# Two-layer hybrid decoder step on one core: product C of the seven-product blocks in the small bank, its `up` made from a copy; three feed-forward blocks on the unnormed input; token mixing's loads and masks issued ahead of its layer norm

## The chip, the core and the metric

One core of a Trainium2 chip runs the whole program once. The metric is the device time of one execution in microseconds (us), and lower is better. The engines are called as the profile calls them: PE is TensorE's matmuls and PEld its weight loads, DVE is VectorE, ACT is ScalarE, POOL is GpSimd, and SP issues the DMAs. PE's granted clock is given as a share of 2.4 GHz, so 0.50 is 1.2 GHz.

## The reference, cut to what matters

The model has two layers and 1024 channels. The program computes 544 columns at once: 512 prompt positions and 8 sequences of 4 sampled positions.

```python
h = rmsnorm(x, g1)
# h @ w_in is shared out over four head groups of 256 channels each:
#  A gated delta rule      B short gated convolution
#  C windowed attention    D token mixing
# D: v = LayerNorm(gelu(.)); out = u * (tril(W_s) @ v + b) inside chunks of 128 positions
x = x + concat(A, B, C, D) @ w_out
h2 = rmsnorm(x, g2)
x = x + (silu(causal_dwconv3(h2 @ w_gate)) * (h2 @ w_up)) @ w_down   # 2816 hidden channels
```

## The kernel before, in words

**Matmuls.** An fp32 product is made as three passes of a narrower type. Each operand is split into a high part and a low part, and high times high, low times high and high times low are summed in PSUM. A product of 544 columns is done as two matmuls of 272 columns (`HT`). A weight tile comes by DMA (`wr`, 4 buffers, L709), ACT makes its high part (`wh`, L745, 3 buffers) and DVE its low part (`wl`, L747, 3 buffers).

**What sets the order.** PE's order is written by hand through the class `Order`. The main program is a generator, and the mixers are side generators (`a00`, `a10` for the delta rule, `c0`, `c1` for attention, `d0`, `d1` for token mixing). `Order.run` keeps an estimated time and picks whose step comes next. A side program yields a time or the name of an event, `mark(name, lat)` says when an event counts as ready, and the table `LAT` adds microseconds to single steps. The order of DVE, ACT, POOL and of SP's DMA queue is worked out by the tile framework's scheduler. Each engine, and SP's queue too, then runs its instructions strictly in that order.

**A layer.** It runs through these stages: the token-mixing and attention-value projections (`ptm`); nineteen 128-channel projections (`pj_*`), with the mixers' small matmuls slotted between their groups; the output product (`po`); the feed-forward net. Layer 1 has its mixers at 31 to 229 us and its feed-forward net at 281.5 to 666 us. Layer 2 has them at 689 to 887 and at 941.5 to 1335 us.

**Token mixing (group D).** `normed_dv` (L1525 to L1535) ends the layer norm: DVE scales the five `dvn`/`dvd` tiles (L1531), and POOL multiplies them by the gain and adds the bias (L1532, L1533). A DMA then writes `dvd` out (`o_cvs`, L1534), and the event `dv` is marked. `mix_d` (L1375) waits for that event first. Only then does it load the mixing weights `wmt` and `wm4` and the bias `dbias`, and POOL multiplies the weights by triangular masks (L1379, L1382). The mixing matmuls are `pmx` (prompt) and `pmd` (samples).

**Attention and delta rule.** `psc` are attention scores. They read `ck`, the rotated keys that DVE finishes at L1578. `pvt` are transposes of the delta rule.

**Feed-forward net.** It has 22 blocks of 128 hidden channels, each with a gate product `pgt` and an up product `pup`. There are three kinds of block:

- `raw` multiplies the unnormed input `xs`. DVE scales the results by `rstd` while it copies them out (L1713, L1714, L1716), and DVE multiplies by up at L1719. Blocks 0 and 1 are raw.
- `plain` multiplies normed forms `f1`, `f2`, `f3`, which `Forms.halves` makes on DVE and ACT (L578, L586, L587, L516). ACT copies the gate out of PSUM (L1728, L1729), and DVE multiplies by up at L1734. Blocks 2, 3 and 4 are plain.
- `seven` makes gate and up of one block from seven half-size products instead of eight (chains `pA`, `pB`, `pC`, `pD`). It reads sums of the forms (`Forms.sums`) and sums of the weights, which POOL makes (`wsums`: `s12` from L724 and L725, `s43` from L727 and L726). These sums stand behind the copy `sfo` of block 3 (L1695) on POOL. Blocks 5 to 21 are of this kind.

After some blocks the down products `pdn` run. Two PSUM pools matter here: `mm` (two buffers of two banks each: `pj`, `po`, `pgt`, `pup`, `pdn` and, before the change, `pC`) and `ps` (two buffers of one bank: `pA`, and the mixers' small results). A new product must wait until the engine that reads its buffer's previous tile is done.

Of the kernel before, what the change touches and what calls it, by code (L numbers as in the profile page):

```python
# [12 lines left out]
ALU = mybir.AluOpType  # L13
# [9 lines left out]
T = SEQ + ND  # L23
HT = T // 2
# [4 lines left out]
NK = DM // 128  # L29
EPS = 1e-6  # L30
FGROUPS = [(0, 5), (5, 11), (11, 17), (17, 22)]
RAW, PLAIN = 2, 5
P0 = 512 - HT


# [238 lines left out]
def _unhost(r):  # L274
# [8 lines left out]
    def conv(a, k, n):  # L283
# [19 lines left out]

LAT = {
    "a00": {
        3: 1.60, 13: 15.62, 14: 3.75, 15: 2.87, 16: 1.87, 17: 3.23, 18: 1.78, 19: 2.03, 34: 1.52,
    },
    "a01": {
        3: 3.96, 4: 1.12, 10: 2.64, 24: 0.84,
    },  # L310
    "a10": {
        3: 1.56, 13: 15.67, 14: 3.68, 15: 2.79, 16: 3.85, 17: 1.45, 25: 1.33, 36: 0.47, 42: 1.13,
    },
    "a11": {
        3: 3.59, 6: 3.32, 13: 1.06, 28: 0.70, 35: 0.30,
    },
    "c0": {
        1: 1.19, 2: 4.34, 5: 7.17, 6: 0.65, 7: 2.67, 8: 3.40,
    },
    "c1": {  # L320
        1: 0.81, 2: 4.06, 5: 7.68, 6: 0.61, 7: 15.38, 10: 1.48,
    },
    "d0": {
        4: 6.53,
# [90 lines left out]
def _body(ctx, tc, I, O, depth=DEPTH, dump=None):  # L415
# [6 lines left out]
    stt = dve.scalar_tensor_tensor  # L422
    od = Order()

    def mm(out, lhsT, rhs, **kw):
        k, m, n = lhsT.shape[0], lhsT.free_size(), rhs.free_size()
        if lhsT.dtype == F32R:
            c = max(n, 256) / 2400.0 + 0.0025
        else:
            c = 4 * max(n, m) / 2400.0  # L430
            if k <= 32 and m <= 32:
                c *= 0.74
            elif k <= 64 and m <= 64:
                c *= 0.72
        od.spend(c, n * k / 128.0 * (1 if lhsT.dtype == F32R else 4))
        nc.tensor.matmul(out, lhsT, rhs, **kw)  # L436
# [9 lines left out]
    def bc(ap, axis, n):  # L446
        u = ap.unsqueeze(axis)
        shp = list(u.shape)
        shp[axis] = n
        return u.to_broadcast(shp)  # L450
# [16 lines left out]
    def n5(nm, w=571):  # L467
        return p5.tile([128, w], F32, tag="w5", name=nm)

    def nx(nm, shape, dt=F32):  # L470
        return slabs.tile(shape, dt, tag="s5", name=nm)

    def ncc(nm, shape):
        return pc.tile(shape, F32, tag="c2", name=nm)
# [4 lines left out]
    def ps(nm, shape):  # L479
        return pss.tile(shape, F32, tag="ps", name=nm)  # L480

    def psmm(nm):
        return pmm.tile([128, 1024], F32, tag="mm", name=nm)
# [16 lines left out]
    def C(nm, a=None, b=None):  # L500
        o, n = _COFF[nm]
        if a is None:
            return cst[:, o:o + n]
        return cst[:, o + a:o + b]
# [280 lines left out]
    def dmp(nm, ap):  # L785
        if dump is not None and nm in dump:
            nc.gpsimd.dma_start(dump[nm], ap)

    def bs(ap):
        return ap.rearrange("p (b t) -> p b t", b=DB)  # L790
# [582 lines left out]


    def mix_d(l, L):  # L1375
        yield ("ev", f"dv{l}")
        wmt = nx("wmt", [128, 4, 128])
        nc.sync.dma_start(wmt, I["wmt"][l])
        pool.tensor_tensor(wmt, wmt, bc(C("tri"), 1, 4), op=ALU.mult)  # L1379
        wm4 = ncc("wm4", [32, 4, 32])  # L1380
        nc.sync.dma_start(wm4, I["wm4"][l])
        pool.tensor_tensor(wm4, wm4, bc(C("udc")[0:32], 1, 4), op=ALU.mult)  # L1382
        dbias = ncc("dbias", [128, 2, 128])
        nc.sync.dma_start(dbias, I["dbias"][l])
        for i in range(2):
            yield ("ev", f"u{l}{i}")
            pmx = ps("pmx", [128, 4, 128])
            for n in range(4):
                for a in range(2):
                    gr = 2 * i + a  # L1390
                    mm(pmx[hs[a], n], L.dvn[n // 2][:, n % 2, 64 * gr:64 * gr + 64], wmt[:, gr],
                       start=True, stop=True)
            pmd = ps("pmd", [128, ND])
            for a in range(2):
                gr = 2 * i + a
                mm(pmd[hs[a]], L.dvd[0:ND, 64 * gr:64 * gr + 64], wm4[:, gr], start=True, stop=True,
                   tile_position=(0, 64 * a))
            mx_ = n5("mx_", T)
            tt(mx_[:, 0:SEQ].rearrange("p (n t) -> p n t", n=4), pmx, bc(dbias[:, i], 1, 4), op=ALU.add)
            tt(bs(mx_[:, SEQ:T]), bs(pmd), bc(dbias[:, i, 0:DS], 1, DB), op=ALU.add)  # L1400
            tt(mx_, mx_, L.du[i], op=ALU.mult)
            dmp(f"od{i}", mx_)
            L.cat[6 + i] = split(mx_, f"d{i}")
            yield 1.0
        od.mark(f"catD{l}", 3.5)


    def main():
# [7 lines left out]
        def xk(k):  # L1416
            return xr[k // 2][:, k % 2, :]
# [33 lines left out]
        for l in range(depth):  # L1451
# [53 lines left out]
            for c in range(5):  # L1505
# [5 lines left out]
                dv = dvn[c // 2][:, c % 2] if c < 4 else dvd[0:ND]  # L1511
# [15 lines left out]
            def normed_dv():  # L1527
                yield ("ev", f"nd{l}")
                with tc.issue_after(L.du_ins):
                    for c, (dv, r0) in enumerate(dvs):  # L1530
                        ts(dv, dv, mv[0:r0, c, 0:1], rs[0:r0, c:c + 1], op0=ALU.subtract, op1=ALU.mult)  # L1531
                        pool.tensor_tensor(dv, dv, lnr[0:r0, 0], op=ALU.mult)  # L1532
                        pool.tensor_tensor(dv, dv, lnr[0:r0, 1], op=ALU.add)  # L1533
                nc.sync.dma_start(O["cvs"][l], dvd[0:ND])  # L1534
                od.mark(f"dv{l}", 8.0)  # L1535

            od.spawn(normed_dv(), f'n{l}')
            yield 0.0
# [199 lines left out]
            def seven(f):  # L1738

                B11, B21, B22, N1, N2, T3, N4 = fm.parts()  # L1740
                K = NK // 2
                a_ = ps("pA", [128, HT])
                b_ = psa.tile([128, HT], F32, tag="pa1", name="pB")
                d_ = psa.tile([128, HT], F32, tag="pa0", name="pD")
                sn = pd.tile([128, 4, HT], F32, tag="d5", name="sn")
                pb, dec = gate_in(f)
                n = SEQ - HT
                w = wnext()
                yield from chain(a_, w, 0, B11)
                act(sn[:, 0], a_, AF.Copy)  # L1750
                yield from chain(b_, w, K, B21)
                tt(pb[:, 2:2 + HT], b_, sn[:, 0], op=ALU.add)
                w = wnext()
                yield from chain(d_, w, 0, N1)
                act(sn[:, 1], d_, AF.Copy)
                yield from chain(a_, w, K, N2, start=False)
                act(sn[:, 2], a_, AF.Copy)
                w = wnext()
                yield from chain(d_, w, 0, B22, start=False)
                tt(pb[:, 2 + HT:2 + SEQ], d_[:, 0:n], sn[:, 2, 0:n], op=ALU.add)  # L1760
                tt(dec[:, :, 2:6], bs(d_[:, n:HT]), bs(sn[:, 2, n:HT]), op=ALU.add)  # L1761
                sl = gate_out(f, pb, dec)
                yield from chain(a_, w, K, T3, start=False)
                act(sn[:, 3], a_, AF.Copy)
                up = n5("up", T)
                stt(up[:, HT:T], a_, -1.0, sn[:, 1], op0=ALU.mult, op1=ALU.subtract)
                c_ = psmm("pC")[:, 0:HT]
                yield from chain(c_, wnext(), 0, N4)
                tt(up[:, 0:HT], c_, sn[:, 3], op=ALU.subtract)  # L1769
                tt(sl, sl, up, op=ALU.mult)  # L1770
                hid[f] = split(sl, "hd")
                yield 0.0

            for kind, i, f0, f1 in FFN_ORDER:
                if kind == "plain":
                    yield from raw(i, i == 0) if i < RAW else plain(i)
                    if i == 0:
                        for kp in range(NK // 2):
                            fm.halves(kp)
                    elif i == RAW:  # L1780
                        with tc.issue_after(fm.end.ins):
                            fm.sums()
                    continue
                if kind == "seven":
                    yield from seven(i)
                    continue
                m, last = i, f1 == NF
                hd = [hid[f] for f in range(f0, f1)]
                if last and l + 1 == depth and m >= NK - 2:
                    if m == NK - 2:  # L1790
                        yield from finale(xk, xr, nnrm, hd)
                    continue
                p = psmm("pdn")
                yield from gemm(p, wnext(), hd)
                tt(xk(m), xk(m), pflat(p), op=ALU.add)  # L1795
                if last:
                    if l + 1 < depth:
                        nx_xs.append(xsplit(xk(m), P(l + 1, "n1g", m, m + 1)))
                    nnrm.feed(m, xk(m))
                    if l + 1 == depth:  # L1800
                        act(xk(m), xk(m), AF.Copy, scale=fng[:, m:m + 1])
                yield 0.0
# [51 lines left out]
```

## Time and profile before

| what | value |
|---|---|
| median of 3 runs | 1336.76 us (1336.02 to 1337.26) |
| the profiled execution's own time | 1336.89 us |
| its span, first to last instruction | 1335.1 us |
| mean granted clock | 0.990 |
| PE busy | 1291.5 us (97%), 12574 matmuls |
| DVE busy | 958.9 us (72%) |
| ACT busy | 647.2 us (48%) |
| POOL busy | 401.9 us (30%) |

Busy shares are means over the span, and a wait is counted at the engine that waits. "[1.31 <-DVE ck L1578]" behind a row says that the engine stood idle for 1.31 us before it, and that DVE's write of `ck` at line 1578 ended that. The sum of PE's busy time holds slow stretches too: a matmul at clock 0.50 is busy for longer.

### The profile page before, as it was taken

Reading aid. Unit: us, or ns where it says so; the run is one execution under the profiler, and the core shown is the slowest. Engines: PE = TensorE matmul, PEld = TensorE weight load, DVE = VectorE, ACT = ScalarE, POOL = GpSimd, SP = SyncE. Lnnn points to the kernel's source line nnn. Section 1 sums busy time; section 2 is a strip of 40 time slices with the busy share of each in tenths; the row PEclk is TensorE's granted clock in tenths of the full one; section 3 lists DMA queues with packets and bytes.
Section 4 is the critical chain, followed back from the end, with each engine's and each line's share of the span. In section 5 each row is a group of like instructions: output and inputs, shape, how many; then the busy total and the mean of one; then the engine's idle time right before and its main releaser. Section 6 shows DMA issues by size and latency. Waiting matters only on the chain.

```text
span 1335.1 us, 29979 instructions
## 1 busy us (share of the span) xinstructions
PE 1291.5 (97%) x12574; PEld 1240.5 (93%) x12574; DVE 958.9 (72%) x1565; ACT 647.2 (48%) x1142; POOL 401.9 (30%) x528
## 2 busy tenths in 40 slices
PE   8998999999999999999999989999999999999997
PEld 7987889999999999999999878889989999999997
DVE  6897943579777778876658867546796887687665
ACT  6645423455455444544545543335555454455444
POOL 2123320001655354452001142100034654643321
PEclk9998999998999999999999989999999999999999
DMA  7222241231233233233532221413312332232232
GB/s 279 99 69 65 80 133 42 89 101 58 70 101 101 84 100 102 84 95 88 162 124 101 66 75 60 124 46 98 99 52 87 92 111 86 97 99 88 89 91 73
DMA packets 48086, 125.60 MB, mean 94 GB/s; under 512 B 10144, under 2 KB 14432, under 8 KB 47824
## 3 DMA queue, kind: packets, MB, share of 16 engines
q1 hardware_dynamic: 47952, 123.70, 29.6%
q8 instruction: 98, 1.61, 0.5%
q14 instruction: 36, 0.29, 0.1%
HBM read 115.01 MB, written 8.67 MB: 93 GB/s over the span
## 4 chain that ended last, share of the span: by engine, by line
PE 81%; DVE 11%; ACT 3%; issue 2%; DMA 1%; POOL 0%; SPq 0%; DVEq 0%; ACTq 0%; POOLq 0%
PE pdn L436 17%; PE pA L436 11%; PE po L436 8%; PE pD L436 7%; PE pup L436 4%; PE pgt L436 4%; PE pB L436 4%; PE pC L436 3%; DVE wl L747 3%; PE ptm L436 2%; PE pj_b L436 2%; PE pj_z L436 2%; PE pj_c L436 2%; PE pj_h L436 2%; PE p L436 2%
## 5 line engine op out<-in xcount | busy, mean ns | idle before, releaser
L747 DVE TENSOR_TENSOR wl<-wr,wh 128x1024 fp32r<-128x1024 f32 (+4 forms) x218 | 257.6, 1182 | 91.0 <-ACT wh L745 89.7
L745 ACT ACTIVATE wh<-wr 128x1024 fp32r<-128x1024 f32 (+4 forms) x218 | 194.1, 890 | 197.6 <-PE pA L436 31.0
L436 PE MATMUL pdn<-hdh,wh 128*128 128x272 f32 x684 | 142.3, 289 | 8.3 <-DVE up L1769 3.7
L436 PE MATMUL pdn<-hdl,wh 128*128 128x272 f32 x684 | 141.7, 288 | 0.5 <-DVE hdl L516 0.5
L436 PE MATMUL pdn<-hdh,wl 128*128 128x272 f32 x684 | 141.2, 288 | 0.0
L745 ACT ACTIVATE wh<-s 128x1024 fp32r<-128x1024 f32 x68 | 72.0, 1058 | 99.9 <-PE pdn L436 90.1
L724 POOL TENSOR_TENSOR s<-wr 128x512 f32<-128x512 f32 x34 | 49.7, 1463 | 228.4 <-DMA wr<-w_u 122.7
L436 PEld LDWEIGHTS pdn<-hdh,wh 128*128 128x128 f32 x684 | 107.1, 188 | 10.2 <-issue 4.4
L436 PEld LDWEIGHTS pdn<-hdl,wh 128*128 128x128 f32 x684 | 107.3, 188 | 0.9 <-DVE hdl L516 0.9
L436 PEld LDWEIGHTS pdn<-hdh,wl 128*128 128x128 f32 x684 | 107.3, 188 | 0.0
L809 DVE SCALAR_TENSOR_TENSOR cacc<-pbf,prm,cacc 128x560 f32<-128x560 f32 x88 | 82.3, 936 | 34.0 <-ACT cacc L807 33.4
L747 DVE TENSOR_TENSOR wl<-s,wh 128x1024 fp32r<-128x1024 f32 x68 | 92.0, 1353 | 8.9 <-ACT wh L745 8.4
L1694 POOL COPY sfo<-pbf 128x2 f32<-128x2 f32 x44 | 27.9, 635 | 151.6 <-DVE pbf L1760 76.2
L1795 DVE TENSOR_TENSOR xr<-xr,pdn 128x544 f32<-128x544 f32 x62 | 44.4, 715 | 40.2 <-PE pdn L436 40.2
L725 POOL TENSOR_TENSOR s<-wr,s 128x512 f32<-128x512 f32 x34 | 62.2, 1831 | 0.9
L807 ACT ACTIVATE cacc<-pbf,prm 128x560 f32<-128x560 f32 x44 | 33.6, 765 | 50.4 <-DVE pbf L1761 45.9
L726 POOL TENSOR_TENSOR s<-wr,s 128x512 f32<-128x512 f32 x34 | 57.4, 1688 | 1.4
L727 POOL TENSOR_TENSOR s<-wr 128x512 f32<-128x512 f32 x34 | 56.7, 1668 | 0.0
L800 POOL MEMSET pbf<- 128x2 f32 x44 | 4.3, 97 | 158.6 <-DVE sq L536 153.6
L516 DVE TENSOR_TENSOR hdl<-sl,hdh 128x544 fp32r<-128x544 f32 x44 | 40.1, 911 | 5.2 <-ACT hdh L515 5.2
L1700 ACT ACTIVATE sl<-cacc 128x512 f32<-128x512 f32 x44 | 27.6, 628 | 32.7 <-DVE cacc L809 32.4
L436 PE MATMUL pA<-f5h,wh 128*128 128x272 f32 x136 | 39.3, 289 | 0.0
(636 smaller groups left out, 4180.4 us busy)
## 6 DMA issues: line engine op xcount, KB each, us to landing
wr<-w_g SPq DMA_DIRECT2D x44, 512.0 KB
wr<-w_u SPq DMA_DIRECT2D x44, 512.0 KB
wr<-w_ch SPq DMA_DIRECT2D x38, 512.0 KB
wr<-w_d SPq DMA_DIRECT2D x32, 384.0 KB
wr<-w_d SPq DMA_DIRECT2D x32, 320.0 KB
wr<-w_o SPq DMA_DIRECT2D x12, 384.0 KB
xr<-x_in SPq DMA_DIRECT2D x7, 544.0 KB
wr<-w_tm SPq DMA_DIRECT2D x8, 392.0 KB
```

The costliest lines, as they stand in the source:

```text
L436: nc.tensor.matmul(out, lhsT, rhs, **kw)
L516: tt(lo, src, hi.bitcast(F32), op=ALU.subtract)
L724: add(s12[:, lo_], u[:, lo_], u[:, hi_], op=ALU.add)
L725: add(s12[:, hi_], g[:, lo_], s12[:, lo_], op=ALU.add)
L726: add(s43[:, lo_], g[:, hi_], s12[:, hi_], op=ALU.add)
L727: add(s43[:, hi_], g[:, lo_], u[:, lo_], op=ALU.add)
L745: act(hi, r, AF.Copy)
L747: tt(lo, r, hi.bitcast(F32), op=ALU.subtract)
L807: act(acc[:, 0:out_n], pb[:, 0:out_n], AF.Copy, scale=wcol[:, 0:1])
L809: stt(acc[:, 0:out_n], pb[:, j:j + out_n], wcol[:, j:j + 1], acc[:, 0:out_n], op0=ALU.mult, op1=ALU.add)
L1694: pool.tensor_copy(sfo[:, f, 0:2], pb[:, SEQ:SEQ + 2])
L1795: tt(xk(m), xk(m), pflat(p), op=ALU.add)
```

## The change

The change does four things:

- `RAW` goes from 2 to 3, so block 2 becomes raw. The sums of the forms are still asked for after block 2.
- `LAT` asks for `psc` (steps 1 of `c0` and `c1`) and `pvt` (step 12 of `a00` and `a10`) somewhat later.
- `mix_d` loads and masks its weights when it is spawned, ahead of its wait for the layer norm. `dv` counts as ready 11 us after it is marked, not 8.
- In `seven`, the second half of `up` is made from the SBUF copy `sn[:, 3]` of product A, no longer from PSUM, and product C goes to the pool `ps`.

```diff
-RAW, PLAIN = 2, 5
+RAW, PLAIN = 3, 5
...
     "a00": {
-        3: 1.60, 13: 15.62, ...
+        3: 1.60, 12: 0.70, 13: 15.62, ...
     "a10": {
-        3: 1.56, 13: 15.67, ...
+        3: 1.56, 12: 0.70, 13: 15.67, ...
     "c0": {
-        1: 1.19, 2: 4.34, ...
+        1: 2.60, 2: 4.34, ...
     "c1": {
-        1: 0.81, 2: 4.06, ...
+        1: 2.30, 2: 4.06, ...
...
     def mix_d(l, L):
-        yield ("ev", f"dv{l}")
         wmt = nx("wmt", [128, 4, 128])
         nc.sync.dma_start(wmt, I["wmt"][l])
         pool.tensor_tensor(wmt, wmt, bc(C("tri"), 1, 4), op=ALU.mult)
...
         nc.sync.dma_start(dbias, I["dbias"][l])
+        yield ("ev", f"dv{l}")
         for i in range(2):
...
-                od.mark(f"dv{l}", 8.0)
+                od.mark(f"dv{l}", 11.0)
...
                 act(sn[:, 3], a_, AF.Copy)
                 up = n5("up", T)
-                stt(up[:, HT:T], a_, -1.0, sn[:, 1], op0=ALU.mult, op1=ALU.subtract)
-                c_ = psmm("pC")[:, 0:HT]
+                stt(up[:, HT:T], sn[:, 3], -1.0, sn[:, 1], op0=ALU.mult, op1=ALU.subtract)
+                c_ = ps("pC", [128, HT])
...
-                    elif i == RAW:
+                    elif i == RAW - 1:
                         with tc.issue_after(fm.end.ins):
                             fm.sums()
```

**SP's queue in layer 1, while the second head pair's projections run.** `wr` are projection weights, `o_sao` and `o_cvs` are outputs that wait for POOL. This is one piece of the difference.

```order
 L709 DMA wr<-w_ch 128x1024
+L1380 DMA wm_1343<-wm 32x128
+L1383 DMA dbias<-dbias 128x256
+L1377 DMA wmt<-wmt 128x512
 L1598 DMA o_sao<-sao 128x162
-L709 DMA wr<-w_ch 128x1024
-L1381 DMA wm_1581<-wm 32x128
-L1384 DMA dbias<-dbias 128x256
-L709 DMA wr<-w_ch 128x1024
+L709 DMA wr<-w_ch 128x1024 x2
 L1534 DMA o_cvs<-dvd 32x256
-L1378 DMA wmt<-wmt 128x512
```

The load of `wmt` moved from behind `o_cvs` to ahead of `o_sao`, past two loads of projection weights.

**POOL in layer 1 at the same place.** `dvn` and `dvd` are the layer norm's tiles, `sao` an output copy. This is one piece of the difference.

```order
+L1381 TENSOR_TENSOR wm_1343<-wm_1343,cst 32x128
+L1378 TENSOR_TENSOR wmt<-wmt,cst 128x512
 L1554 COPY sao<-pb 128x3
 L1555 COPY sao<-pb 128x24
 L1532 TENSOR_TENSOR dvn_221<-dvn_221,lnr 128x256 x2
 L1532 TENSOR_TENSOR dvn_222<-dvn_222,lnr 128x256
-L1533 TENSOR_TENSOR dvn_221<-dvn_221,lnr 128x256
-L1382 TENSOR_TENSOR wm_1581<-wm_1581,cst 32x128
-L1533 TENSOR_TENSOR dvn_221<-dvn_221,lnr 128x256
+L1533 TENSOR_TENSOR dvn_221<-dvn_221,lnr 128x256 x2
```

Both masks now stand ahead of the layer norm's instructions. Before, the mask of `wmt` stood behind the last of them.

**ACT at blocks 3 and 4 of layer 1's feed-forward net.** `wh<-s` is the high part of POOL's weight sum `s12`, and the `pgt` behind it is block 4's. First before, then now.

```order
L745 ACTIVATE wh<-wr 128x1024
L1700 ACTIVATE sl<-cacc 128x512
L1701 ACTIVATE sl<-cacc 128x32
L515 ACTIVATE hdh<-sl 128x544
L745 ACTIVATE wh<-s_4548 128x1024
L1728 ACTIVATE pbf<-pgt 128x512
L1729 ACTIVATE pbf<-pgt 128x8x4
```

```order
L745 ACTIVATE wh<-wr 128x1024
L515 ACTIVATE f5h<-fv 128x544 x2
L1700 ACTIVATE sl<-cacc 128x512
L1701 ACTIVATE sl<-cacc 128x32
L745 ACTIVATE wh<-s_4549 128x1024
L1728 ACTIVATE pbf<-pgt 128x512
L1729 ACTIVATE pbf<-pgt 128x8x4
```

In both kernels block 4's gate leaves PSUM behind the split of `s12`. Half of the `f5h` splits moved between the two weight splits, and `hdh` moved behind.

## Rows read from the trace of the kernel before

**Rows 1.** The page: busy times, the chain that ended last.

```profile
PE 1291.5 (97%) x12574; PEld 1240.5 (93%) x12574; DVE 958.9 (72%) x1565; ACT 647.2 (48%) x1142; POOL 401.9 (30%) x528
...
PE 81%; DVE 11%; ACT 3%; issue 2%; DMA 1%; POOL 0%; SPq 0%; DVEq 0%; ACTq 0%; POOLq 0%
```

**Rows 2.** PE's waits, all of the span: waited for, us in total, times, longest.

```profile
PE pmx L436 <- POOL wmt L1379: 9.2, 2, 5.5
PE pdn L436 <- DVE up L1769: 3.7, 5, 1.2
...
PE psc L436 <- DVE ck L1578: 2.7, 2, 1.4
...
PE pvt L436 <- DVE kd L1022: 1.1, 2, 0.6
```

**Rows 3.** PE in order of time, both layers' first `pmx`: start, us, instruction, [idle before <-releaser].

```profile
122.60 1.98 PE L436 MATMUL pmx<-wmt,dvn 128*64 128x128 f32 x16 [5.54 <-POOL wmt L1379]
...
777.76 1.09 PE L436 MATMUL pmx<-wmt,dvn 128*64 128x128 f32 x16 [3.64 <-POOL wmt L1379]
```

**Rows 4.** SP's queue in order of time, layer 1.

```profile
95.14 0.37 SPq L709 DMA_DIRECT2D wr<-w_ch  x1
...
117.87 0.34 SPq L1534 DMA_DIRECT2D o_cvs<-dvd  x1
118.31 0.36 SPq L1378 DMA_DIRECT2D wmt<-wmt  x1
```

**Rows 5.** POOL in order of time at the layer norm, layer 1, then layer 2's last.

```profile
102.56 1.28 POOL L1554 COPY sao<-pb 128x3 f32<-128x3 f32 x1 [7.88 <-DVE pb L1552]
...
117.13 0.71 POOL L1533 TENSOR_TENSOR dvd<-dvd,lnr 32x256 f32<-32x256 f32 x1
121.28 1.26 POOL L1379 TENSOR_TENSOR wmt<-wmt,cst 128x512 f32<-128x512 f32 x1 [3.44 <-DMA wmt<-wmt]
...
774.79 0.71 POOL L1533 TENSOR_TENSOR dvd<-dvd,lnr 32x256 f32<-32x256 f32 x1
```

**Rows 6.** Windows at `pmx`: stretch, length, busy PE, PEld, DVE, ACT, POOL, clock, DMA, GB/s.

```profile
120.00:132.00 12.00, 8.96 (x112) 6.99 (x114) 4.19 (x6) 4.53 (x8) 2.71 (x2) 0.57 0.16 53
776.00:788.00 12.00, 9.27 (x127) 6.77 (x128) 5.83 (x11) 4.59 (x9) 3.16 (x4) 0.72 0.16 48
```

**Rows 7.** Windows of the mixers in layer 1, and of `pgt` and `pup` of block 2.

```profile
61.00:170.00 109.00, 100.75 (x1434) 91.22 (x1434) 93.07 (x199) 54.93 (x118) 34.48 (x62) 0.95 0.23 71
...
305.90:318.30 12.40, 10.82 (x52) 9.21 (x51) 11.33 (x19) 6.43 (x14) 0.00 (x0) 0.72 0.15 49
318.30:324.30 6.00, 6.00 (x50) 6.00 (x49) 5.05 (x10) 3.01 (x7) 1.16 (x4) 1.00 0.24 87
...
965.90:977.50 11.60, 9.03 (x51) 6.92 (x51) 11.34 (x19) 6.30 (x14) 0.00 (x0) 1.00 0.16 50
```

**Rows 8.** POOL in order of time, before the first seven-product block, both layers.

```profile
331.68 3.43 POOL L1694 COPY sfo<-pbf 128x2 f32<-128x2 f32 x1 [8.48 <-ACT pbf L1728]
...
341.26 1.78 POOL L725 TENSOR_TENSOR s<-wr,s 128x512 f32<-128x512 f32 x1
...
345.49 0.18 POOL L1694 COPY sfo<-pbf 128x2 f32<-128x2 f32 x1
...
991.41 3.02 POOL L1694 COPY sfo<-pbf 128x2 f32<-128x2 f32 x1 [8.90 <-ACT pbf L1728]
...
1000.43 1.29 POOL L725 TENSOR_TENSOR s<-wr,s 128x512 f32<-128x512 f32 x1
```

**Rows 9.** ACT in order of time at block 4, layer 1.

```profile
343.07 1.06 ACT L745 ACTIVATE wh<-s 128x1024 fp32r<-128x1024 f32 x1 [2.85 <-POOL s L725]
...
344.51 0.19 ACT L1729 ACTIVATE pbf<-pgt 128x32 f32<-128x32 f32 x1
```

**Rows 10.** DVE in order of time at block 1, layer 1.

```profile
301.23 0.68 DVE L1713 TENSOR_TENSOR pbf<-pgt,rstd 128x512 f32<-128x512 f32 x1
...
312.43 0.71 DVE L1719 TENSOR_TENSOR sl<-sl,pup 128x544 f32<-128x544 f32 x1
```

More of the change, by code (lines that the diff above doesn't have):

```diff
@@ L305 @@
     "a00": {
-        3: 1.60, 13: 15.62, 14: 3.75, 15: 2.87, 16: 1.87, 17: 3.23, 18: 1.78, 19: 2.03, 34: 1.52,
+        3: 1.60, 12: 0.70, 13: 15.62, 14: 3.75, 15: 2.87, 16: 1.87, 17: 3.23, 18: 1.78, 19: 2.03, 34: 1.52,
     },
@@ L311 @@
     "a10": {
-        3: 1.56, 13: 15.67, 14: 3.68, 15: 2.79, 16: 3.85, 17: 1.45, 25: 1.33, 36: 0.47, 42: 1.13,
+        3: 1.56, 12: 0.70, 13: 15.67, 14: 3.68, 15: 2.79, 16: 3.85, 17: 1.45, 25: 1.33, 36: 0.47, 42: 1.13,
     },
@@ L317 @@
     "c0": {
-        1: 1.19, 2: 4.34, 5: 7.17, 6: 0.65, 7: 2.67, 8: 3.40,
+        1: 2.60, 2: 4.34, 5: 7.17, 6: 0.65, 7: 2.67, 8: 3.40,
     },
     "c1": {
-        1: 0.81, 2: 4.06, 5: 7.68, 6: 0.61, 7: 15.38, 10: 1.48,
+        1: 2.30, 2: 4.06, 5: 7.68, 6: 0.61, 7: 15.38, 10: 1.48,
     },
```

## The prediction

> **What bounds the kernel now.** I read the page first. PE is busy for 97% of the span and makes 81% of the chain that ended last [rows 1], so time is won only where PE waits or runs slowly. The list of PE's waits [rows 2] then says which: the largest is `pmx` on the mask of `wmt`, 9.2 us in two waits, and the change touches four more kinds in the list. The timeline [rows 3 to 5] tells why `pmx` waits. The load of `wmt` stands in SP's queue behind `o_cvs`, which waits for the layer norm's last instruction on POOL. So the load goes out at 118.31, the mask starts at 121.28, and PE, there since 122.60 - 5.54 = 117.06, starts at 122.60. The windows show the second price: in the 12 us from 120 the granted clock is 0.57, in layer 2 it is 0.72 [rows 6]. After its wait PE ran in part at 1.2 GHz.
>
> **The wait of `pmx`.** The loads now go out right behind the weight load issued at 95.14 [rows 4]. Issue to mask took 121.28 - 118.31 = 3.0 us, and the masks stand on POOL where it was idle for 7.88 us before 102.56 [rows 5]. They end near 100, so the idle time covers them. If that cover were gone, `sao` and the layer norm behind it would start later by a mask's 1.26 us. The two loads and `dbias` each pass two weight loads on SP, and the weight load behind them moves by three issues of about 0.4 us [rows 4]. It still has to wait for a buffer and for `o_sao`, so I cost this at nothing, at most 1.2 us. What is late next is the layer norm itself: before, it ended at 117.13 + 0.71 = 117.84 in layer 1 and at 775.5 in layer 2 [rows 5]. PE will come at 117.06, less its two waits ahead (below, 1.9), plus six projection matmuls that the later `dv` lets in (6.00 us for 50 is 0.12 each [rows 7], so 0.75): 115.9. In layer 2, 777.76 - 3.64 = 774.12 becomes 773.0 [rows 3]. If the layer norm ended as before, PE would wait 1.9 and 2.5 us. It may come earlier, since one mask is gone from between its instructions, so the new wait is 0 to 2.5 us per layer. I count the old wait as gone, -9.2, and put the new one into the term on new waits.
>
> **The clock behind it.** If a stretch at half clock took twice as long, the busy time times what the clock lacked would be the loss: 8.96 x 0.43 = 3.9 us in layer 1 and 9.27 x 0.28 = 2.6 in layer 2 [rows 6], 6.5 in all. `pmx` itself took 1.98 us against 1.09 [rows 3], a little less than double, so I take -5.5. The bounds are 0 (another wait near it pulls the clock down again) and -6.5.
>
> **`psc` and `pvt` later.** They waited 2.7 and 1.1 us, twice each [rows 2]. One group of six matmuls, 0.75 us, more or less in front of each covers the wait of `pvt` (0.55). The waits of `psc` are 1.35 us each and need two groups, which the 1.4 us added in the table buy. I take -3.8; the bounds are 0 and -3.8, because another product on the same `ck` may wait in their place.
>
> **Product C in the small bank.** A down product waits for the reader of `pC`, 3.7 us in five waits [rows 2]. With C out of that pool the down product's buffer was read long before. What is late next are the split weights, which these products wait for elsewhere, so I take -3.0, between 0 and -3.7. `up` from SBUF instead of PSUM is the same instruction on the same size, 34 times on DVE, which is not the bound in this stretch; I cost it at nothing.
>
> **Block 2 raw.** Its gate product took 12.4 us in layer 1 and 11.6 in layer 2 where the up product behind it took 6.00 [rows 7], since DVE made the forms while PE used them. The raw product needs no forms: in the times of before it runs from 305.9 to 311.9. Its copy out of PSUM then stands on DVE behind block 1's L1716 and two form splits, where L1719 was before, at 312.43 [rows 10]; that copy takes 0.68 us [rows 10] and a short second part, about 0.8, so `pup` starts near 313.2, a new wait of 1.3. By six-microsecond steps and one more wait of 0.4 for block 2's up, block 3's gate ends at 325.2 and block 4's at 337.6. Here a new limit stands. Block 4's up product takes the buffer of its own gate, and ACT copies that out behind the high part of `s12`. That split waits for a weight buffer, so for PE nearly through the gate, and takes with the two copies 344.70 - 343.07 = 1.6 us [rows 9]: `pup` starts at 339.2. POOL is the other condition. From `sfo` of block 3 to `s12` it needed 343.04 - 331.68 = 11.4 us [rows 8], and `sfo` started 1.4 behind that gate's end (318.3 + 12 = 330.3); now 325.2 + 1.4 + 11.4 = 338.0, then 1.6, so 339.6. The first seven-product block then starts at 345.6 instead of 318.3 + 30 = 348.3, so -2.7. Layer 2 in the same steps: 965.9 + 6.0 + 1.3 + 12.0 = 985.2, + 1.9 + 10.3 + 1.6 = 999.0, and 1005.0 instead of 1007.5, so -2.5. I take -5.2. The bounds are +3.0 per layer, if the clock falls behind the new waits as it did in the window of layer 1 (10.82 x 0.28 [rows 7]), and -8.6 in all if ACT's copy did not stand behind the split.
>
> One rule bears on POOL. Its copy of 128x2 took 3.43 us at 331.68 and 0.18 at 345.49 [rows 8], so something stopped it. The Trainium skill, page "SBUF — State Buffer", section "SBUF: two separate sides", says that GpSimd and a VectorE instruction with two SBUF inputs exclude each other for a whole instruction. The trace agrees as far as those two rows go. By this rule the raw block's extra L1716, which has the size of the L1719 that took 0.71 us [rows 10], would hold POOL longer, and the sum would be up to 1.4 us higher.
>
> **New waits in the mixers.** PE will run 6 to 9 us ahead of where it was, with ACT and DVE behind it. DVE was busy for 93.07 of the 109 us from 61 to 170 [rows 7]. With 5.5 + 3.9 + 1.9 us less, that is 93.07 of 97.7, or 95%, and a chain of dependent work seldom fills an engine so far. So some of the gain turns into waits on DVE, ACT or the layer norm. Bounds: 0, and the whole 9.4 us of layer 1 with as much again of layer 2's 6.2. I take +3.0 in layer 1 and +1.5 in layer 2, nearer the small end, because PE's waits for DVE ahead of `pmx`, 3.8 us in both layers [rows 2], were small in an equally full stretch.
>
> **Sum.** -9.2 - 5.5 - 3.8 - 3.0 - 5.2 + 4.5 = -22.2 us. The profiled execution took 1336.89, 0.13 above the median, so I predict 1336.76 - 22.2 = 1314.6 us. That is 1.7%, far more than the 0.2% that a measurement of this kernel can tell from no change.
>
> **Rivals.**
> - *The mixers keep up.* No new waits, all of the clock and of product C: -9.2 - 6.5 - 3.8 - 3.7 - 5.2 = -28.4, so 1308.4. For it: DVE idles through much of the 12 us after 120 [rows 6]. Against it: 95%.
> - *Something else takes the place of the mask.* The layer norm on POOL holds `pmx` for 1.9 and 2.5 us, and the clock falls again: 1314.6 + 4.4 + 5.5 = 1324.5; without the clock, 1319. Or DVE paces layer 1's mixers and gives back most of 9.4: 1321. For it: the layer norm ended at 117.84, later than PE will come.
> - *Slower: the weight sums come too late.* POOL works against a DVE that block 2 now loads more. If its chain from `sfo` to `s12` doubles, `s12` is there at 326.6 + 22.8 = 349.4, block 4's up ends at 357.0 instead of 348.3, and the clock falls (3.0): +11.7. In layer 2, 987.1 + 20.6 + 1.6 + 6.0 = 1015.3, +7.8 and +3.0. That is +22.5 against -17.0 for the rest: 1342.3. It decides from 8.5 us lost per layer. For it: the copy that took 3.43 us. Against it: the added work on DVE is 1.5 us per block, and the chain would have to double.
> - *No change.* The terms cancel by chance, or the scheduler's order keeps the loads from leaving early; the order on SP and POOL speaks against the second.
>
> **Chances.** Forecast 0.57 (its own range 1309 to 1319), mixers keep up 0.15, another wait in the mask's place 0.20, weight sums late 0.04, no change 0.04. So faster 0.92, same 0.04, slower 0.04. The range takes in the first three with most of their bounds: 1306 to 1326.
>
> **What would show it.** Right: no wait of `pmx` on L1378's mask, and at most 2.5 us on POOL's L1533; clock 1.00 around the first `pmx`; no `psc` on `ck` and no `pdn` on `up`; block 2's gate 6.0 us long with 1.3 us of wait behind it; block 4's up held 1.6 to 2.5 us by L1729; the first `pA` of layer 1 near 338, which is 348.3 less 2.7 and less 7.8 from the mixers (5.5 + 3.4 of the clock + 1.9 - 3.0). Wrong: a clock near 0.5 in the mixers' middle, a list of new waits on DVE of over 8 us, or `wh` on POOL's L725 holding block 4's up for longer than 3 us.

## The result: 0.6% slower, and the profile after

The changed kernel takes 1346.44 us (median of 5 runs, 1342.37 to 1346.92) against 1337.26 us for the kernel before on the same chip. The ratio is 1.0064, with a 95% interval of 1.0048 to 1.0080. I had forecast 1314.6 us.

The page of the changed kernel shows the same 12574 matmuls in a longer span:

```profile
PE 1296.9 (96%) x12574; PEld 1248.5 (93%) x12574; DVE 977.0 (73%) x1571; ACT 648.6 (48%) x1138; POOL 399.0 (30%) x528
...
PE 84%; DVE 9%; ACT 4%; issue 2%; DMA 0%; DVEq 0%; SPq 0%; ACTq 0%
```

PE is busy for 5.4 us more than before [rows 1]. Part of that is matmuls at half clock: the mean granted clock is 0.983 after 0.990. The list of PE's waits shows what came in place of the waits of before (waited for, us in total, times, longest):

```profile
PE pup L436 <- ACT pbf L1729: 6.6, 2, 3.3
PE pl L436 <- ACT sql L942: 4.4, 1, 4.4
PE pmx L436 <- ACT pt L1363: 4.2, 1, 4.2
PE pR L436 <- ACT Wc L1054: 4.1, 1, 4.1
PE py L436 <- DVE Y L1170: 3.9, 1, 3.9
PE pvt L436 <- DVE vnd L1225: 2.5, 1, 2.5
PE pup L436 <- DVE pbf L1714: 2.5, 2, 1.3
...
PE pkd L436 <- DVE mx__1796 L1399: 1.4, 1, 1.4
```

Three waits of [rows 2] are gone: `pmx` on the mask, `psc` on `ck` and `pdn` on `up`. So are those of `pgt` on the forms. Nine others stand there instead, of 1.4 to 6.6 us; the list leaves out the last, `pA` on ACT's `sn`, 1.4 us in four waits. `pl` makes sums of squares for the norms of queries and keys, which ACT reads as `sql`. `pt` is ACT's copy of the transposed attention scores `ptr`. `pkd`, `py`, `pW` and `pR` are small products of the delta rule, `Wc` is ACT's copy of `pW`, and `mx` are results of token mixing. To see where the time went I compared the start of the same product in both profiled executions:

| start of | before, us | after, us | difference, us |
|---|---|---|---|
| last `pj_u` group, layer 1 | 114.56 | 111.89 | -2.67 |
| first `pmx`, layer 1 | 122.60 | 120.60 | -2.00 |
| second `pmx`, layer 1 | 136.78 | 133.57 | -3.21 |
| first `po`, layer 1 | 226.55 | 233.62 | +7.07 |
| first `pgt`, layer 1 | 281.31 | 287.67 | +6.36 |
| last group of `pgt` of block 4, layer 1 | 341.90 | 344.04 | +2.14 |
| first `pA`, layer 1 | 348.16 | 355.26 | +7.10 |
| first `ptm`, layer 2 | 665.62 | 669.68 | +4.06 |
| last `pj_u` group, layer 2 | 771.62 | 773.29 | +1.67 |
| first `pmx`, layer 2 | 777.76 | 783.96 | +6.20 |
| first `po`, layer 2 | 886.05 | 896.41 | +10.36 |
| first `pA`, layer 2 | 1007.29 | 1019.31 | +12.02 |
| last `pA`, layer 2 | 1291.31 | 1300.91 | +9.60 |

The table reads in stages. Ahead of `pmx` each layer wins 2.4 us (-2.67 in layer 1, of which 0.24 stood there at its first product already, and +4.06 to +1.67 in layer 2). The mixers behind that point lose 9.7 us in layer 1 (-2.67 to +7.07) and 8.7 in layer 2. From the feed-forward net's start to the first `pA` the kernel loses 0.7 and 2.8 us. The seven-product blocks win about 3 and 2.4 us.

**At `pmx`.** PE in order of time, the first `pmx` of layer 1 in the changed kernel:

```profile
120.60 1.97 PE L436 MATMUL pmx<-wmt,dvn 128*64 128x128 f32 x16 [4.23 <-ACT pt L1363]
```

POOL in the same stretch has both the mask and the layer norm ready early, at 100.76 and 115.56:

```profile
99.45 1.31 POOL L1378 TENSOR_TENSOR wmt<-wmt,cst 128x512 f32<-128x512 f32 x1 [1.92 <-DMA wmt<-wmt]
...
114.84 0.72 POOL L1533 TENSOR_TENSOR dvd<-dvd,lnr 32x256 f32<-32x256 f32 x1
```

What PE waits for is a PSUM buffer of the pool `ps`, which ACT must first read as `pt`. On ACT, `pt` stands behind the second `du`:

```profile
116.02 1.28 ACT L1610 ACT_TABLE_LOAD   x1
117.31 0.66 ACT L1610 ACTIVATE du<-du 128x544 f32<-128x544 f32 x1
119.28 0.69 ACT L942 ACTIVATE sql<-pl,cst 128x512 f32<-128x512 f32 x1 [1.31 <-issue]
119.87 0.59 ACT L1363 ACTIVATE pt<-ptr 128x512 f32<-128x512 f32 x1
```

In the kernel before, the same copy stood ahead of that table load:

```profile
115.94 0.58 ACT L1363 ACTIVATE pt<-ptr 128x512 f32<-128x512 f32 x1
116.53 1.28 ACT L1610 ACT_TABLE_LOAD   x1
```

So 4.23 us of the 5.54 us [rows 3] came back from another engine, and the clock fell again. In layer 2 `pmx` itself waits for nothing, but `pl` just ahead of it waits 4.40 us for `sql`, at 781.45. The windows of the changed kernel (stretch, length, busy PE, PEld, DVE, ACT, POOL, clock, DMA, GB/s) show it in both layers, and twice more:

```profile
120.00:132.00 12.00, 11.40 (x194) 8.81 (x195) 6.11 (x10) 4.52 (x9) 0.00 (x0) 0.77 0.10 38
136.00:150.00 14.00, 9.79 (x218) 8.73 (x219) 8.65 (x23) 4.47 (x9) 4.94 (x6) 0.88 0.27 80
...
781.00:793.00 12.00, 11.11 (x128) 8.44 (x128) 5.17 (x9) 5.25 (x11) 0.00 (x0) 0.58 0.13 43
826.00:840.00 14.00, 11.55 (x206) 10.28 (x206) 5.32 (x21) 4.76 (x10) 0.00 (x0) 0.76 0.17 65
...
345.00:357.00 12.00, 9.25 (x62) 9.25 (x63) 9.89 (x14) 6.50 (x13) 2.34 (x4) 0.86 0.15 46
```

The first and third rows answer to [rows 6]: 0.77 for 0.57, and 0.58 for 0.72. The second, fourth and fifth stand behind the new waits of `py`, `pR` and `pup`.

**Behind `pmx`.** PE in order of time, the changed kernel, without the projections' matmuls:

```profile
133.57 1.09 PE L436 MATMUL pmx<-wmt,dvn 128*64 128x128 f32 x16
...
136.30 0.30 PE L436 MATMUL pkd<-kq 64*32 64x64 f32 x2 [1.40 <-DVE mx__1796 L1399]
...
137.17 0.75 PE L436 MATMUL pW<-R,N 32*32 32x32 f32 x64
...
142.80 0.33 PE L436 MATMUL py<-Y,Nd 32*32 32x32 f32 x8 [3.92 <-DVE Y L1170]
...
146.07 0.26 PE L436 MATMUL py<-Y,Nd 32*32 32x32 f32 x8
146.27 1.09 PE L436 MATMUL pk<-kq 64*64 64x128 f32 x16
147.29 1.09 PE L441 MATMUL ptr<-cst,sc 128*128 128x128 f32 x8
148.31 0.75 PE L436 MATMUL pR<-Wc,Tm 32*32 32x32 f32 x64
```

`pkd` feeds a chain on DVE whose result `Y` the product `py` reads. In the kernel before `pkd` started at 139.67 and `py` at 146.63 without a wait, because PE did `pk`, `pR`, `ptr` and projections in those 7 us. Here `py` stands right behind `pW` and six projection matmuls, and the other three products come after it. So PE reaches `py` 2.6 us after `pkd`'s start and waits 3.92.

**At block 4.** ACT in order of time before the first seven-product block, layer 1 of the changed kernel:

```profile
344.66 0.66 ACT L515 ACTIVATE f5h<-fv 128x544 fp32r<-128x544 f32 x1 [0.68 <-DVE fv L607]
...
346.08 1.04 ACT L745 ACTIVATE wh<-s 128x1024 fp32r<-128x1024 f32 x1
347.03 0.58 ACT L1728 ACTIVATE pbf<-pgt 128x512 f32<-128x512 f32 x1
347.51 0.19 ACT L1729 ACTIVATE pbf<-pgt 128x32 f32<-128x32 f32 x1
```

Block 4's gate was done on PE at 344.45, and `pup` starts at 347.75 behind the last of these rows. The split `wh<-s` starts right behind ACT's instruction before it, so POOL's sum was there in time. The `f5h` split shown ahead of it waits for a sum made by DVE (L607).

### The profile page after: what moved, and what is told of

Read it like the earlier page. It is cut to its first block, busy times and chain, and to the rows that moved or that the text cites. A ratio compares the mean times of both kernels' runs of the same rounds, so it can differ in the third digit from the quotient of the medians.

```text
span 1344.8 us, 29982 instructions
## 1 busy us (share of the span) xinstructions
PE 1296.9 (96%) x12574; PEld 1248.5 (93%) x12574; DVE 977.0 (73%) x1571; ACT 648.6 (48%) x1138; POOL 399.0 (30%) x528
## 4 chain that ended last, share of the span: by engine, by line
PE 84%; DVE 9%; ACT 4%; issue 2%; DMA 0%; DVEq 0%; SPq 0%; ACTq 0%
PE pdn L436 19%; PE pA L436 11%; PE po L436 7%; PE pD L436 7%; PE pup L436 4%; PE pB L436 4%; PE pC L436 3%; PE pgt L436 3%; PE pj_z L436 2%; PE ptm L436 2%; PE pj_h L436 2%; PE pj_u L436 2%; DVE wl L747 2%; PE pj_b L436 2%; PE pj_c L436 2%
## 5 line engine op out<-in xcount | busy, mean ns | idle before, releaser
L809 DVE SCALAR_TENSOR_TENSOR cacc<-pbf,prm,cacc 128x560 f32<-128x560 f32 x88 | 74.7, 849 | 32.0 <-ACT cacc L807 31.5
L747 DVE TENSOR_TENSOR wl<-s,wh 128x1024 fp32r<-128x1024 f32 x68 | 88.9, 1307 | 3.1 <-ACT wh L745 2.8
L515 ACT ACTIVATE hdh<-sl 128x544 fp32r<-128x544 f32 x44 | 28.9, 656 | 28.1 <-DVE sl L1770 21.3
L516 DVE TENSOR_TENSOR hdl<-sl,hdh 128x544 fp32r<-128x544 f32 x44 | 39.1, 889 | 3.0 <-ACT hdh L515 3.0
L436 PE MATMUL pA<-f1h,wh 128*128 128x272 f32 x136 | 39.6, 291 | 1.4 <-ACT sn L1764 1.4
```

The lines of the kernel that those rows point to most:

```text
L515: act(hi, src, AF.Copy)
L516: tt(lo, src, hi.bitcast(F32), op=ALU.subtract)
L747: tt(lo, r, hi.bitcast(F32), op=ALU.subtract)
L809: stt(acc[:, 0:out_n], pb[:, j:j + out_n], wcol[:, j:j + 1], acc[:, 0:out_n], op0=ALU.mult, op1=ALU.add)
```

## The experiments

All ratios are against the kernel before, timed on the same chip in the same rounds. Its median there was 1337.3 to 1338.9 us.

**One part at a time.** The kernel before with one of the four parts.

```diff
 # s1_mix: loads, masks and bias ahead of the event, later dv
     def mix_d(l, L):
-        yield ("ev", f"dv{l}")
...
+        yield ("ev", f"dv{l}")
...
-                od.mark(f"dv{l}", 8.0)
+                od.mark(f"dv{l}", 11.0)
```

> The kernel before with token mixing's part alone: loads and masks ahead of the layer norm, dv 11 us after its mark. Theory T (this part loses: the first pmx loses its 9.2 us on the mask but waits for other PSUM readers on ACT, 4 us in layer 1, and the mixers behind it wait for DVE and ACT): 1339 to 1347 us. Rival L (the later psc and pvt of the table are at fault, this part alone keeps its gain): 1322 to 1328 us.

1330.65 us, ratio 0.9935 (0.9915 to 0.9955), between the two ranges. `pmx` waits for nothing, and none of the waits on `pt` or `Y` is there. The part that I suspected first is a gain of 0.65%: theory T falls, and rival L had put the gain too high.

```diff
 # s2_lat: the table alone
 a00, a10:  + 12: 0.70
 c0:  - 1: 1.19   + 1: 2.60
 c1:  - 1: 0.81   + 1: 2.30
```

> The kernel before with the table's part alone: psc and pvt later. Theory T: psc and pvt win about 2.4 us in each layer ahead of pmx, but pmx then still waits for the mask until the same moment, so 1335 to 1338 us. Rival L (the later scores push the attention chain and with it the mixers behind): 1340 to 1346 us.

1349.14 us, ratio 1.0077 (1.0053 to 1.0101): the loss that rival L named, and 3 us more than its range. The waits are the new ones, with the old wait for the mask beside them:

```profile
PE pmx L436 <- POOL wmt L1379: 8.0, 1, 8.0
PE pmx L436 <- ACT pt L1363: 7.0, 1, 7.0
...
PE py L436 <- DVE Y L1170: 3.6, 1, 3.6
```

```diff
 # s3_pc: product C and up alone
-                stt(up[:, HT:T], a_, -1.0, sn[:, 1], op0=ALU.mult, op1=ALU.subtract)
-                c_ = psmm("pC")[:, 0:HT]
+                stt(up[:, HT:T], sn[:, 3], -1.0, sn[:, 1], op0=ALU.mult, op1=ALU.subtract)
+                c_ = ps("pC", [128, HT])
```

> The kernel before with the seven-product part alone: up from the copy, product C in the small bank. Theory T: down products no longer wait for up, 3.0 and 2.4 us as between the two traces' stages, so 1331 to 1333 us. Rival (what was won there came from the shifted start of the stage): 1336 to 1338 us.

1330.47 us, ratio 0.9940 (0.9922 to 0.9957), a little more than expected. Of the waits of `pdn` over 0.5 us only one kind is left, at the last down products:

```profile
PE pdn L436 <- ACT hdh L515: 1.6, 2, 0.8
```

Both the 3.7 us on `up` and the 2.9 us on `wh`, which I had left in place, are gone: 6.6 us together, which is most of the 8.4 by the medians. The run changes both lines together; it doesn't say what each is worth.

```diff
 # s4_raw: the third raw block alone
-RAW, PLAIN = 2, 5
+RAW, PLAIN = 3, 5
...
-                    elif i == RAW:
+                    elif i == RAW - 1:
```

> The kernel before with the third raw block alone. Theory T: the forms' stall goes, but block 4's up waits 3.3 us for its own gate's copy behind the split of s12, with a stretch at half clock: +0.7 and +2.8 us as between the two traces' stages, so 1339 to 1342 us. Rival (that wait comes from the mixers' shift, or from product C): 1330 to 1334 us.

1337.78 us, ratio 0.9998 (0.9986 to 1.0010): no change, and outside both ranges. Its trace has the two waits of `pup` on L1729 with the mixers and product C as before, so these waits belong to this part:

```profile
PE pup L436 <- ACT pbf L1729: 6.7, 2, 3.3
```

In the profiled execution, which was the longest of the ten (1341.97 us), the way from the first `pgt` to the first `pA` is longer by 0.9 and 3.0 us, near theory T's +0.7 and +2.8. The median shows no such loss.

The four alone make -8.2, +10.3, -8.4 and -1.1, which is -7.4 by sum. Together they made +9.2.

**All but the table.**

```diff
 # s5_nolat: the changed kernel with LAT as it was
```

> The changed kernel with the table LAT as before: early loads, product C in the small bank and the third raw block stay. Theory T2 (the table's lines alone are at fault; run alone they cost 10 us, and the early loads and product C won about 7 to 8 each alone): 1320 to 1326 us, no wait of py on Y and no pmx on pt. Rival I (the parts also get in each other's way without the table): 1329 to 1336 us.

1324.27 us, ratio 0.9895 (0.9877 to 0.9913). The table costs 22 us on top of the other parts, more than the 10 us it costs alone. The wait of `py` on `Y` is gone, and so is that of `pmx` on `pt`.

```diff
 # s6_mixpc: s5_nolat with
-RAW, PLAIN = 3, 5
+RAW, PLAIN = 2, 5
```

> Early loads and product C alone: neither the table's lines nor the third raw block. Theory T2: the raw block alone was worth nothing, so the same as with it, 1320 to 1326 us. Rival (the raw block wins with PE running ahead): 3 to 5 us slower than with the raw block.

1321.35 us, ratio 0.9873 (0.9853 to 0.9892). The raw block is worth nothing here either; without it the kernel is even 3 us better.

**Which line of the table.**

```diff
 # s8_latc: the kernel before with the lines c0 and c1 alone
```

> The kernel before with the two lines c0 and c1 alone (psc later), pvt's lines as before. Theory T2c (later scores reorder the chain so that py follows pkd without other small matmuls between): 1344 to 1350 us, as with all four lines. Rival T2a (pvt's lines do it): 1335 to 1338 us.

1339.73 us, ratio 1.0010 (0.9998 to 1.0022): T2c falls. One of the waits shows here already, though: in layer 2 `pmx` waits 3.1 us for `pt`.

```diff
 # s9_lata: the kernel before with the lines a00 and a10 alone
```

> The kernel before with the lines a00 and a10 alone (pvt later), psc's lines as before. Theory T3 (only both pairs of lines together move py right behind pkd on PE; with this pair alone ptr, pk and pR still stand between them): 1334 to 1341 us. Rival T2a (pvt's lines alone do the harm): 1345 to 1350 us.

1333.84 us, ratio 0.9971 (0.9957 to 0.9986). T2a falls too, and T3 fits, with a time 0.2 us under its range: neither pair alone costs time that these runs can tell. The listing of PE's order in layer 1 agrees. With one pair alone `ptr`, `pk` and `pR` stand between `pkd` and `py`, as before; with both, in the changed kernel, only `pW` and projections do:

```
 before                         both pairs
 pkd                            pkd
 pj_h                           pW
 pk                             pj_h
 pR                             py
 pj_h                           pj_h
 ptr                            py
 pj_h                           pk
 py                             ptr
```

The reason, as I read the code of `Order` (no run prints its times): the step of `decode_a` that issues `py` asks for 1.5 us after `pkd` and has no entry of its own in `LAT`. In the kernel before other side steps were due ahead of it, and they filled the 7 us. With both pairs later those steps are not yet due, so `Order` takes `py` after the 1.5 us.

```diff
 # s10_py: the changed kernel, with py asked for later
     "e0": {
-        4: 6.92,
+        4: 6.92, 5: 4.50,
     "e1": {
-        4: 3.69,
+        4: 3.69, 5: 4.50,
```

> The changed kernel, with one more entry for e0 and e1 in the table: py is asked for 4.5 us later, so that pk, ptr and pR stand between pkd and py again. Theory T3: layer 1 loses its wait of py on Y (3.9 us) and the half clock behind it, 4 to 8 us by the projections' end, and 1336 to 1342 us in all, since layer 2's waits on ACT stay. Rival (the small matmuls' order doesn't matter, DVE and ACT pace this stretch): the wait turns up at the next product and the time stays at 1344 to 1348 us.

1334.04 us, ratio 0.9969 (0.9956 to 0.9982). One number, added for each layer, takes 12.4 us off the changed kernel, more than expected. PE in order of time, this run:

```profile
138.07 0.75 PE L436 MATMUL pW<-R,N 32*32 32x32 f32 x64
...
141.21 1.09 PE L436 MATMUL pk<-kq 64*64 64x128 f32 x16
142.23 1.09 PE L441 MATMUL ptr<-cst,sc 128*128 128x128 f32 x8
143.25 0.75 PE L436 MATMUL pR<-Wc,Tm 32*32 32x32 f32 x64
...
145.64 0.26 PE L436 MATMUL py<-Y,Nd 32*32 32x32 f32 x8
```

`pk`, `ptr` and `pR` are back in the gap and `py` waits for nothing. The 2.5 us of `pvt` on `vnd` behind it are gone too. The window answers to the 0.88 above:

```profile
136.00:150.00 14.00, 12.81 (x287) 10.84 (x287) 10.39 (x27) 6.49 (x17) 5.39 (x8) 1.00 0.27 81
```

In layer 1 the first `po` starts at 225.11 instead of 233.62, so 8.5 us come from layer 1's mixers. The waits on `pt`, `sql` and `Wc` stay, 4.2, 4.4 and 3.8 us.

**The remaining 10 us of the table.**

```diff
 # s13_latc_in: the changed kernel without the lines a00 and a10
```

> The changed kernel without the two pvt lines: psc's lines, early loads, product C and the third raw block stay. Theory T3 (only both pairs together spoil the order): 1320 to 1328 us. Rival (later scores alone keep pmx waiting for pt once the mask no longer does): 1330 to 1340 us, with pmx on pt of 3 us or more.

1328.55 us, ratio 0.9930 (0.9914 to 0.9946).

```diff
 # s14_lata_in: the changed kernel without the lines c0 and c1
```

> The changed kernel without the two psc lines: pvt's lines stay. Theory T3: 1318 to 1328 us. Rival (the pvt lines move a product ahead of its data once PE is early): 1330 to 1340 us.

1326.21 us, ratio 0.9912 (0.9897 to 0.9926). Beside 1324.27 without any of the lines, one pair costs 4.3 us and the other 1.9, both 22.2. The second run is inside T3's range, the first lies between T3's and its rival's. In both, `ptr`, `pk` and `pR` stand between layer 1's `pkd` and `py`. The wait of `pl` on `sql` comes with either pair (4.5 and 3.3 us). Those of `pmx` on `pt` and of `pR` on ACT's late `Wc` are in neither list, so here they need both pairs; in the kernel before, `psc`'s lines alone were enough for 3.1 us of `pmx` on `pt`.

**The start of the seven-product blocks.**

```diff
 # s7_fix: s5_nolat, with ACT's order set at block 4
-                act(dec[:, :, 2:6], bs(pflat(p, SEQ, T)), AF.Copy)
+                e = act(dec[:, :, 2:6], bs(pflat(p, SEQ, T)), AF.Copy)
...
+                if f == PLAIN - 1:
+                    with tc.issue_after(e.ins):
+                        w = wnext()
```

> As the changed kernel with the old table, and ACT told to split s12 only after it has copied block 4's gate out of PSUM. If block 4's up waits 3.3 us only for that split ahead of the copy: the wait falls to 0.5 us or less in each layer and the half clock behind it goes, so 6 to 10 us below the same kernel without it. If POOL's sum or PE's own buffer sets that moment: no more than 1 us.

1320.67 us, ratio 0.9869 (0.9851 to 0.9888): 3.6 us less, where 6 to 10 were expected. The wait fell from 3.3 to 2.4 us per layer, so the split's 1.06 us was only one part. ACT in order of time in this run shows the other:

```profile
329.32 0.66 ACT L515 ACTIVATE f5h<-fv 128x544 fp32r<-128x544 f32 x1 [3.42 <-DVE fv L607]
...
331.38 0.66 ACT L515 ACTIVATE f5h<-fv 128x544 fp32r<-128x544 f32 x1 [0.44 <-DVE fv L607]
332.71 0.66 ACT L515 ACTIVATE f5h<-fv 128x544 fp32r<-128x544 f32 x1 [0.68 <-DVE fv L607]
...
334.62 0.19 ACT L1729 ACTIVATE pbf<-pgt 128x32 f32<-128x32 f32 x1
```

ACT stands behind the `f5h` splits, which wait for DVE's sums. DVE in the same run, at 323 us and 8 us later:

```profile
323.13 1.53 DVE L607 TENSOR_TENSOR fv<-hn 128x272 f32<-128x272 f32 x1
324.58 1.81 DVE L516 TENSOR_TENSOR f4l<-fu,f4h 128x544 fp32r<-128x544 f32 x1
...
330.91 0.43 DVE L607 TENSOR_TENSOR fv<-hn 128x272 f32<-128x272 f32 x1
331.26 0.71 DVE L516 TENSOR_TENSOR f4l<-fu,f4h 128x544 fp32r<-128x544 f32 x1
```

```diff
 # s11_small: s5_nolat, up of blocks 2 and 4 as two tiles in the small banks
+    def small(nm):
+        return [ps(nm, [128, HT]), psa.tile([128, HT], F32, tag="pa0", name=nm)]
...
-                pu = psmm("pup")
+                pu = small("pup") if f == RAW - 1 else psmm("pup")
...
-                pu = psmm("pup")
+                pu = small("pup") if f == PLAIN - 1 else psmm("pup")
```

> Early loads, product C in the small bank and the third raw block with the old table, and the up products of blocks 2 and 4 as two tiles in the small banks, so that they wait for no reader of a gate. If those two buffers are what holds the start of the seven-product blocks: pup's waits of 1.3 and 3.3 us per layer go, with the half clock: 1311 to 1317 us. If DVE's sums or POOL's pace the start: the wait moves to the first pA or its weights, 1321 to 1325 us.

1323.82 us, ratio 0.9898 (0.9882 to 0.9914). `pup` waits for nothing, and the first `pA` starts at 337.67 instead of 344.60. But then:

```profile
PE pD L436 <- DVE sl L768: 9.8, 2, 4.9
```

`pD` takes the bank that the up product held, and DVE reads that late. The 4.6 us per layer of `pup` turned into 4.9 of `pD`.

```diff
 # s12_both: s11_small with s7_fix's order on ACT
```

> The same with ACT told to split s12 behind the copy of block 4's gate. If the up product no longer needs that gate's buffer, the order of the two on ACT is worth nothing: within 2 us of the run without it, 1311 to 1317 us. If the copy is still waited for (by the convolution of block 4 and the first seven-product block): 2 to 4 us faster than without it.

1323.62 us, ratio 0.9899 (0.9879 to 0.9918): the same as without it.

```diff
 # s15_f5late: s7_fix, with the second loop of Forms.sums run behind the copy
+                if f == PLAIN - 1:
+                    with tc.issue_after(e.ins):
+                        fm.late()
```

> As the run with the old table and ACT's order set (1320.7 us), and the f5 forms, which only the seven-product blocks need, asked for behind the copy of block 4's gate. If the copy was late because ACT stood behind f5 splits whose sums DVE had not yet made (2.3 us of wait left): 1314 to 1318 us, with pup's wait under 1 us. If DVE paces the start whatever the order: the wait moves to pD on its form, 1319 to 1324 us.

1321.99 us, ratio 0.9884 (0.9868 to 0.9900), no better than without it. The wait of `pup` grew back to 3.5 us, now on DVE's product of block 3:

```profile
PE pup L436 <- DVE sl L1746: 6.9, 2, 3.5
```

Three ways of freeing a buffer moved the wait from ACT to DVE and from `pup` to `pD`. One of them, ACT's order, won 3.6 us; the others won nothing (1321.99 against 1320.67, and 1323.82 against 1324.27). This speaks for DVE as what paces the stretch, but no run makes DVE's work there shorter, so it isn't shown. DVE is itself held up: while POOL makes the weight sums, DVE's four instructions from 323.13 in s7_fix take 1.53, 1.81, 1.52 and 1.53 us, and the same four forms from 329.93 take 0.71 or 0.43 us each. In sum the first four take 4.4 us more, where `pup` waits 2.4 us in this run and 3.3 in the changed kernel. Whether the wait goes when POOL's sums and DVE's sums are kept apart was not tried.

Of all versions `s7_fix` (1320.67 us) and `s6_mixpc` (1321.35 us) are fastest. Their intervals overlap, and both beat the kernel before by 1.3%.

## Why the prediction was wrong, point by point

- **The step that failed: "`psc` and `pvt` later".** I took -3.8 us, bounded it by 0 and -3.8, and allowed no loss. With the other parts it cost 22.2 us. That is 26.0 of the 31.8 us between forecast and result; without the table's lines the kernel took 1324.27 us, where the other terms alone make 1318.4. The waits themselves went as forecast: 2.4 us per layer were won ahead of `pmx`. But the table is read by a planner, and a later step changes which steps are due behind it. I looked at the order of SP, POOL and ACT and not at PE's own behind `pmx`, where `py` had moved right behind `pkd`. Of the 22.2 us 12.4 came back by asking for `py` later; the rest stands beside the waits on `pt`, `sql` and `Wc`, which were not removed one by one.
- **The wait of `pmx`.** Loads and masks left early as forecast: the mask ended at 100.76, and the layer norm at 115.56 instead of 117.84, so it held nobody. The 4.2 us in layer 1 came from ACT's order, which I had not listed as what is late next. Without the table's lines the step was right: `pmx` waited for nothing in s1_mix. With the clock, and with what the mixers give back, this part was worth 8.2 us, where my terms made 14.7 less 4.5.
- **The clock behind it.** Sound in s5_nolat (mean 0.995 for 0.990), undone in the changed kernel by the new waits (0.983).
- **New waits in the mixers.** I took 4.5 us and argued from DVE's busy share. In the changed kernel the waits of `pl`, `pR`, `py`, `pvt` and `pkd` are 4.4 + 4.1 + 3.9 + 2.5 + 2.3 = 17.2 us, and a busy share does not tell of those: in 136 to 150 DVE was busy for only 8.65 of 14 us. They came with the table's order, not from DVE's load: in s5_nolat, without the table, DVE was busy for 12.46 of the 14 us from 136, and of these waits only 0.9 us of `pl` and 0.8 of `pR` are left.
- **Product C.** Right in direction and too small: -8.4 us by the medians instead of -3.0, since the waits of `pdn` on `wh` went too. The move has a small price that I had not listed: `pA` waits for ACT's `sn`, 0.8 us in all in s3_pc.
- **Block 2 raw.** I took -5.2 and measured -1.1, with an interval that takes in no change; beside the early loads and product C it cost 2.9 us (1324.27 against 1321.35). Block 2's gate and the 1.3 us of `pup` behind it came as worked out. The 1.6 us that I gave block 4's up behind ACT were 3.3: I had counted the split and the copies, but not the `f5h` splits ahead of them, nor what slowed the sums that these wait for. The clock fell behind it to 0.86.
- **The rivals.** The one on the other side, weight sums that come too late on POOL, did not happen: the split of `s12` did not wait for POOL. The rival that something else takes the place of the mask named the layer norm and DVE; it was ACT, and only with the table's lines.

What stays open: why ACT's `pt`, `sql` and `Wc` come late with the table's lines, and why the two pairs together cost so much more than each. The runs show that it is so, but not which step of the planner does it.

## What to carry to other kernels

A number in a planner's table is not a local edit: print the changed order of the engine that bounds the kernel, and look for a product that now stands close behind the one that feeds it. Test the parts of a change one by one and then all but one. Here the three other parts together gained 1.0%, two of them alone 1.3%, and the fourth turned the whole into a loss. And where a cure for a wait moves it on without moving the time, look next at the engine that stands behind all of these waits, and at what slows that engine.

## What I had not expected of the hardware

POOL was slowed beside DVE in the kernel before: its copy of 128x2 took 3.43 us from 331.68 [rows 8], while DVE's L602 and L607 took 0.43 us each from 331.24. DVE is slowed beside POOL too. In s7_fix the 272-column L607 took 1.53 us at 323.13 and 0.43 at 330.91, and the 544-column L516 1.81 and 0.71. POOL was busy for all of the 3 us from 323, and for 0.35 of the 3 us from 330. The first and the last of its weight sums in this stretch:

```profile
322.87 1.49 POOL L724 TENSOR_TENSOR s<-wr 128x512 f32<-128x512 f32 x1
...
327.62 1.37 POOL L726 TENSOR_TENSOR s<-wr,s 128x512 f32<-128x512 f32 x1
```

The rule that I cited from the Trainium skill, page "SBUF — State Buffer", section "SBUF: two separate sides", holds for both engines, and these rows agree with it. In the sum I had used it against POOL alone. In the changed kernel the same L607 and L516 take 1.54 and 1.81 us from 335.05 on, beside the same weight sums, ahead of the wait of `pup` for block 4.
